# DeltaNet stage of a two-layer decoder step: GpSimd's copies, products and subtractions go to VectorE and ScalarE

## The chip, the cores and the metric

One core of one Trainium2 chip runs the whole step as one program. The metric is device time in microseconds (us) of that program, the median of several runs. Engines are called by the profile's names: PE is TensorE (PEld its weight loads), DVE is VectorE, ACT is ScalarE, POOL is GpSimd, and SP issues all DMAs of this kernel.

## What is computed

A prompt of 256 tokens and 8 sample sequences of 4 tokens go through two decoder layers together (288 columns). Layer 1 mixes its tokens with a gated DeltaNet: 16 heads of 128 x 128, a short convolution on q, k and v, and a chunked form with a triangular inverse. Only this layer is touched. Cut from the reference:

```python
qkv, new_buf = causal_dwconv(qkv, conv_buf, conv_w, None)      # width 4, with the last 3 rows kept
qkv = silu(qkv); q, k, v = split(qkv)                          # 16 heads of 128 each
q = l2norm(q) * DK ** -0.5; k = l2norm(k)
A = where(strict, (k * beta) @ k^T * dec, 0) + I               # per head and chunk
sol = triangular_solve(A, [v * beta, k * beta * exp(gc)])
def step(S, inp):
    v_new = vw_c - kcd_c @ S
    o = qg_c @ S + attn_c @ v_new
    S = S * gl_c[..., None, None] + kg_c^T @ v_new             # the state's update
```

For the samples the state has 8 blocks of 128 x 128 per head (one per sequence), each with its own decay gl.

## The kernel before

**Precision and weights.** Every projection takes operands split into a high and a low part. `wsplit` makes the parts of at most 512 weight columns: ACT copies the high part (`wh`), then the low part `wl = raw - wh` is a subtraction on DVE, or, for every third piece (`pool_share` is 3, counter `wn`), on POOL (L386). PE takes three matmuls of 288 columns per 128 weight columns: `xH,wh`, `xL,wh`, `xH,wl`. The pieces are made a few ahead of their use: five `wh` and five `wl` buffers.

**The DeltaNet stage.** `gdn` runs 16 heads as five streams of jobs: `inputs` (four projections and the convolutions, the filler), `prepare` (transposes, norms, decay products), `invert` (the triangular inverse, `inverse`), `sample` and `sample2` (the 8 sample states), and `chain` (the two prompt chunks). `flow` writes PE's order by hand from a table of latencies, so PE takes its steps in a fixed order and waits in it. The order of DVE, ACT, POOL and SP is set by the framework's scheduler from the program and its own costs. After head 8 the first half of the output projection (`out_half`) joins the filler.

**What POOL does in the stage.** A third of the `wl` pieces; the convolution's small copies in `evac_pad` (history into the padded row `pad`, new history into `osc`, L596 to L600); copies of the sample columns of q and k into `KQx` (L1538, L1539); in `inverse` half of the mask products `at`, the products `a8t`, `sx` and the subtraction `lo`, and the two copies into `X` (L729, L730); the scaling of the sample state `S0` by its decays, one product of 128 x 1024 per head (L1627); the spread of `US` to `UX`, one product of 96 x 1024 per head (L1644); the powers of -0.5 in `rsqrt_small` (L345); zeroing of `pad`; and two of the eight `xL` subtractions in `out_half`.

**The sample state.** `S0` is loaded, read by PE against `KQx`, scaled by POOL, and later gets two PSUM banks of 128 x 512 added (`p_row`, L1653 and L1654) before it is stored. The tag `row` has one PSUM bank.

Of the kernel before, what the change touches and what calls it, by code (L numbers as in the profile page):

```python
# [42 lines left out]
# ---------------------------------------------------------------- host: layout and shape constants  # L43
def _consts():
# [37 lines left out]
    # halved on the chip  # L82
    ("w0", 8), ("a0", 8), ("ka", 8), ("sw", 48), ("sb", 12), ("gw", 192), ("gnorm", 1),
    # as they come
# [24 lines left out]
def _wt(w, pad=None):  # L109
    """(K, C) -> [col tile, 128, ktile*128]"""  # L110
    w = np.asarray(w)
    K, C = w.shape
    return np.ascontiguousarray(w.reshape(K // 128, 128, C // 128, 128).transpose(2, 1, 0, 3)).reshape(
        C // 128, 128, K)
# [8 lines left out]
def _tok(a):  # L123
    """(tokens, features) -> [128, ftile, tokens]"""
    a = np.asarray(a)
    n, f = a.shape
    return np.ascontiguousarray(a.T.reshape(f // 128, 128, n).transpose(1, 0, 2))


def layout(i):  # L130
# [44 lines left out]
    # (b, h, v, k) -> [pair, (half of the sequences, k), (head, sequence of the half), v]  # L175
# [3 lines left out]
    # (b, h, p, n) -> [b, n, h*64+p]  # L179
# [3 lines left out]
    # (b, h, k, v) -> [h, k, b, v]  # L183
# [46 lines left out]
# ---------------------------------------------------------------- the program  # L230
# [19 lines left out]
class K:  # L250
    def __init__(self, tc, ctx, d):
# [10 lines left out]
        self.pe_us, self.step = 0.0, None  # L262
        self.wready = []
        self.wplan()

    # -- small things
    def gt(self, nm="gt"):
        """short-lived [128, N]"""
        return self.mp.tile([128, N], F32, name=nm, tag="gt", bufs=self.ngt)

    def gn(self, nm="gn"):
        """the same, of a later stage"""
        return self.mp.tile([128, N], F32, name=nm, tag="gn", bufs=2)

    def gw(self, nm="gw"):
        """the same for padded rows"""
        return self.mp.tile([128, 320], F32, name=nm, tag="gw", bufs=self.ngw)

    def P(self, tag=None):
        """a PSUM bank; self.pt names the current stage's banks"""  # L280
# [3 lines left out]
    def PA(self):  # L284
        """one of all eight banks"""
# [4 lines left out]
    def reserve(self, pads, dls, gws, gts):  # L290
        """the row buffers come first in a pool: they are free first"""
# [18 lines left out]
    def tr(self, out, a, r=slice(0, 128)):  # L310
        """out = a transposed; a lies on the partitions r"""
# [20 lines left out]

    def rsqrt(self, y, x, t):
        """y = 1/sqrt(x): y, x, t tile views of one shape, on VectorE"""
# [7 lines left out]
    def rsqrt_small(self, y, x):  # L342
        """the same for a few columns, on GpSimd"""
# [3 lines left out]
    def split(self, hi, lo, x, gain=None, eng=None):  # L347
        """hi + lo = x*gain exactly, each in 12 significant bits"""
# [7 lines left out]
    def stack(self, out, x, twin=0, eng=None):  # L356
        """x [32, n] as 96 rows that contract against those of another such x to a product of full
        precision: hi, lo, hi, or for the other one (twin) hi, hi, lo"""
# [13 lines left out]
    # -- weights  # L372
# [7 lines left out]
    def wsplit(self, raw):  # L380
        """at most WC columns of raw as hi, lo"""
# [9 lines left out]
    def wplan(self):  # L391
        """the weights of all projections, in their order: (w, ktiles[, M[, k0]])"""
# [19 lines left out]
    def wcut(self, w, kts, M=128, k0=0):  # L412
        """loads of at most 1024 columns, split in parts of at most WC"""
# [11 lines left out]
    def wnext(self):  # L425
        """the next part of the planned weights as name, hi, lo; the parts after it are on their way"""
# [7 lines left out]
    def proj_g(self, w, hi, lo, kts, M=128, n=N, ps=None, start=True, stop=True):  # L434
        """psum[:M, :n] = sum over ktiles of w[ktile].T @ (hi + lo)[ktile], w: the next of the plan"""
# [24 lines left out]
    # -- several streams of work side by side, in the order in which TensorE shall take them  # L460
    def weave(self, *streams):
        """advance the (name, generator[, most weight]) streams together, each at its own even pace;
        a generator yields the weight of its last step (None: 1)"""
# [13 lines left out]
    def flow(self, *streams):  # L477
        """streams of jobs side by side, in the order in which TensorE shall take their steps. A job is
        (kind, key, generator function, keys of the jobs that come before it); the first stream fills
        the time in which no step of the others has its operands. LAT says when that is: for each kind  # L480
        of job, how long after its start or the step before the operands of a step come, in us"""
# [60 lines left out]
    # -- norms  # L542
# [21 lines left out]
    def last_norm(self, sq):  # L564
        """1/rms by token from sacc and sq, on all partitions of a PSUM bank"""
# [23 lines left out]
    # -- padded projections  # L589
    def evac_pad(self, ps, H, hist, out_state, zero=True):  # L590
        """psum * r into [H zeros | prompt | per sequence: H history, 4 tokens]; state out"""
# [4 lines left out]
        self.g.tensor_copy(smp[:, :, 0:H], hist)  # L596
        self.tt(p[:, H:H + NP], pr(ps), pr(self.rB), MUL)
        self.tt(smp[:, :, H:], sa(ps), sa(self.rB), MUL)
        self.g.tensor_copy(out_state[:, 0:H], p[:, NP:NP + H])
        self.g.tensor_copy(out_state[:, H:].rearrange("p (b t) -> p b t", t=H), smp[:, :, T:])  # L600
        return p, w, smp

    def shift(self, ps, i, out):
        """token shift of projection tile i -> out [128, N]"""
# [9 lines left out]
    def conv_silu(self, ps, hist, out_state, wcols, bias, out, out2=None):  # L614
        """causal conv of width 4 (weights and bias halved) and silu -> out [128, N]"""
# [16 lines left out]
    def softplus(self, x, r, tl):  # L632
        """x[r] <- softplus(x[r]); tl(): temp views of x's shape"""
# [15 lines left out]
    # -- (I - A)^-1, A strictly lower, given A^T; unit matrices side by side in the free dimension  # L649
    def inverse(self, AT, n, top, XT, tag, bank):  # L650
        """AT, XT: [128, n, 128] views; returns the transposed inverse in XT. top: last level.
        The blocks of 32 on the diagonal lie as [128, n, 32], and have a tile of TensorE each"""
# [9 lines left out]
        def times(l, r, w=1):  # L662
            """l^T r, block by block, in a bank"""
# [10 lines left out]

        at, a8t, ac, a8, lo = small("at"), small("a8t"), small("ac"), small("a8"), small("lo")
        sx, mx = small("sx", 2), small("mx", 2)
        m8 = bc(self.c("m8"), sc, 1)
        for i, u in enumerate(q):
            self.tt(at[u], AT[u, :, u], bc(self.c("up")[u], [32, n, 32], 1), MUL, self.g if i % 2 else None)
        self.v.transpose(out=fl(ac), in_=fl(at))  # L680
        self.tt(a8t, at, m8, MUL, self.g)
        self.tt(a8, ac, m8, MUL)
        self.tt(sx[:, :, 32:64], a8, bc(self.c("id32"), sc, 1), ADD, self.g)
        self.tt(lo, ac, a8, SUB, self.g)
        # inside blocks of 8: (1 + A)(1 + A^2)(1 + A^4)
# [14 lines left out]
        # of blocks of 8 in 32: with M = X A', (1 + M)(1 + M^2) X  # L700
# [16 lines left out]
        # blocks of 32 in pairs  # L717
# [9 lines left out]
        if wide:  # L727
            X = self.X64
            self.g.tensor_copy(X[q[0], :, q[0]], xc[q[0]])  # L729
            self.g.tensor_copy(X[q[1], :, q[1]], xc[q[1]])  # L730
# [13 lines left out]
        # the halves  # L744
# [13 lines left out]
    def inverse4(self, AT, n, XT, X, tag, bank):  # L758
        """the same for 4x4 diagonal blocks of n 32x32 matrices on 32 partitions"""
# [24 lines left out]
    # ------------------------------------------------------------ layer 0: RWKV-7  # L784
    def rwkv(self):
# [8 lines left out]
        # the second half of h is not in use yet  # L794
# [21 lines left out]
        def head():  # L816
# [3 lines left out]
            # as 128 rows hi, hi and 64 of lo  # L820
# [9 lines left out]
        def inputs(j, o):  # L830
            """projections of pair j"""
# [5 lines left out]
        def prepare(j, o):  # L837
# [3 lines left out]
            # rows hi, lo of the first map; lo, hi of the second  # L841
# [4 lines left out]
            # kappa = k * k_k stays without its norm; 1/|kappa|^2 scales by token  # L846
# [50 lines left out]
            # rows (half of the sequences, k)  # L897
# [10 lines left out]
            # products inside a chunk: rows (b | k) for the first head, (k | b) for the second  # L908
# [13 lines left out]
            # bonus  # L922
# [10 lines left out]
        def sample(j, o):  # L933
            """token-major copies; one block of 8 sequences of 4"""
# [37 lines left out]
            # rows that meet only their half of the sequences  # L972
# [20 lines left out]
        def sample2(j, o):  # L993
# [21 lines left out]
            # rows hi, lo  # L1015
# [17 lines left out]
        def centre(y, n, rr, va):  # L1033
            """y - its mean over the head, by token; va: variance"""
# [9 lines left out]
        def chain(j, o, prev):  # L1044
            """chunks in order; y token-major, rows (first head | second head)"""
# [67 lines left out]
    # ------------------------------------------------------------ layer 0: SSD  # L1113
    def transpose3(self, p, src):
        """[128, N] -> token-major in p: two prompt tiles and p[:32, 256:384]"""
# [4 lines left out]
    def seq_ends(self, out, x):  # L1120
        """out = (value at the end of its chunk or sequence) - x, on x's partitions"""
# [5 lines left out]
    def end_factors(self, x, tag):  # L1127
        """x [16, N] cumulated logs -> [128, 16, 9]: exp at the ends of prompt chunk 1 and of the sequences"""
# [13 lines left out]
    def row_parts(self, rows, tag="rowp", bufs=1):  # L1142
        """rows 32..48 of the prompt as hi, lo for products that repeat one of them on all partitions,
        and the columns that choose row h"""
# [10 lines left out]
    def sample_decay(self, rows, r0, TOKs):  # L1155
        """[32 s, 16 h, 32 l]: exp(c_l - c_s) inside a sequence for s <= l, else 0; c in rows r0.. of rows"""
# [11 lines left out]
    def ssd(self):  # L1168
# [33 lines left out]
        def first():  # L1202
            """dt and the decay sums; B and C"""
# [5 lines left out]
            # softplus by token, in fewer columns  # L1209
# [26 lines left out]
        def groups():  # L1236
            """B and C"""
# [102 lines left out]
        def group(g, os):  # L1340
# [4 lines left out]
            for b in range(B):  # L1345
                if b % 2 == 0:
                    h2 = al("h0", [128, 2, 512], "Gm")
                    self.load(h2, d["sssd"][b:b + 2, :, gs].rearrange("b p x -> p b x"))
                    # by turns on two blocks of the columns
# [48 lines left out]
    def ssd_gate(self, j):  # L1398
        """silu of z, twice, waits in DRAM"""
# [7 lines left out]
    def layer0(self):  # L1407
        """both groups of heads; the second one's projections fill the end of the first one's chain"""
# [41 lines left out]
    # ------------------------------------------------------------ layer 1: gated DeltaNet  # L1450
    def gdn(self):
# [25 lines left out]
        # beta, decay sums  # L1477
# [37 lines left out]
        def inputs(h, o):  # L1515
            """projections of head h"""
# [18 lines left out]
        def prepare(h, o):  # L1535
            KQ = o.KQ
            kqv = KQx.rearrange("p (b x) -> p b x", x=68)
            self.g.tensor_copy(kqv[:, :, 0:4], sa(KQ[:, 0, :]))  # L1538
            self.g.tensor_copy(kqv[:, :, 32:36], sa(KQ[:, 1, :]))  # L1539
            # k token-major, decays and products inside a chunk  # L1540
# [588 lines left out]
```

## Time and profile before

| | |
|---|---|
| median of 3 runs | 3469.5 us (3468.0 to 3475.63) |
| profiled execution, span | 3472.1 us |
| PE busy in the span | 3343.0 us (96%) |
| DVE, ACT, POOL busy | 2259.5 us (65%), 1653.4 us (48%), 1394.1 us (40%) |
| the DeltaNet stage in the profiled execution | about 1754 to 2466 us |

The profiled execution has no time of its own beside its span of 3472.1 us; it lies 2.6 us above the median. PE's busy time is modelled from pipelined matmuls. A wait names the instruction that ended it. The DeltaNet stage is the 712 us between the first matmuls of its projections and the last head's end.

### The profile page before, as it was taken

Reading aid. Unit: us, or ns where it says so; the run is one execution under the profiler, and the core shown is the slowest. Engines: PE = TensorE matmul, PEld = TensorE weight load, DVE = VectorE, ACT = ScalarE, POOL = GpSimd, SP = SyncE. Lnnn points to the kernel's source line nnn. Section 1 sums busy time; section 2 is a strip of 40 time slices with the busy share of each in tenths; the row PEclk is TensorE's granted clock in tenths of the full one; section 3 lists DMA queues with packets and bytes.
Section 4 is the critical chain, followed back from the end, with each engine's and each line's share of the span. In section 5 each row is a group of like instructions: output and inputs, shape, how many; then the busy total and the mean of one; then the engine's idle time right before and its main releaser. Section 6 shows DMA issues by size and latency. Waiting matters only on the chain. (4 is left out here: it accounts for less than half of the span.)

```text
span 3472.1 us, 73636 instructions
## 1 busy us (share of the span) xinstructions
PE 3343.0 (96%) x27952; PEld 3154.0 (91%) x27952; DVE 2259.5 (65%) x4775; ACT 1653.4 (48%) x3623; POOL 1394.1 (40%) x1899
## 2 busy tenths in 40 slices
PE   8989999899999999999999999999999999999998
PEld 6878788788999999999988888887989999999998
DVE  8666667775765366446577877888667654663563
ACT  6544445544544344444545555555454444443444
POOL 6444443543433233233435444444434332332333
PEclk9999999999999999999999999999999999999999
DMA  7522223566445544554643444444654455455554
GB/s 235 192 89 96 79 92 118 170 211 223 157 166 164 165 164 166 166 166 165 188 140 130 137 137 135 132 135 136 213 205 165 164 166 167 165 165 165 165 167 144
DMA packets 194818, 547.23 MB, mean 158 GB/s; under 512 B 33824, under 2 KB 60064, under 8 KB 194464
## 3 DMA queue, kind: packets, MB, share of 16 engines
q1 hardware_dynamic: 194464, 542.52, 48.0%
q8 instruction: 220, 3.60, 0.4%
q14 instruction: 134, 1.10, 0.1%
HBM read 511.58 MB, written 30.86 MB: 156 GB/s over the span
## 5 line engine op out<-in xcount | busy, mean ns | idle before, releaser
L304 PE MATMUL p_acc<-xH,wh 128*128 128x288 f32 x6464 | 1971.9, 305 | 5.9 <-ACT xH L329 3.8
L304 PE MATMUL p_acc<-xL,wh 128*128 128x288 f32 x6464 | 1919.9, 297 | 3.7 <-DVE xL L316 3.6
L304 PE MATMUL p_acc<-xH,wl 128*128 128x288 f32 x6464 | 1916.4, 296 | 4.1 <-DVE wl L316 4.0
L329 ACT ACTIVATE wh<-raw 128x512 fp32r<-128x512 f32 x1755 | 1094.7, 629 | 1157.7 <-PE p_acc L304 1015.0
L316 POOL TENSOR_TENSOR wl<-raw,wh 128x512 fp32r<-128x512 f32 x585 | 772.6, 1321 | 1334.6 <-ACT wh L329 1289.4
L304 PEld LDWEIGHTS p_acc<-xH,wh 128*128 128x128 f32 x6464 | 1221.1, 189 | 35.4 <-issue 11.6
L304 PEld LDWEIGHTS p_acc<-xH,wl 128*128 128x128 f32 x6464 | 1226.0, 190 | 6.9 <-DVE wl L316 5.2
L304 PEld LDWEIGHTS p_acc<-xL,wh 128*128 128x128 f32 x6464 | 1223.8, 189 | 7.9 <-DVE xL L316 4.9
L316 DVE TENSOR_TENSOR wl<-raw,wh 128x512 fp32r<-128x512 f32 x1170 | 855.4, 736 | 529.9 <-ACT wh L329 503.5
L316 DVE TENSOR_TENSOR pad<-p_acc,rB 128x256 f32<-128x256 f32 x348 | 92.3, 299 | 92.7 <-PE p_acc L304 92.1
L316 POOL TENSOR_TENSOR sacc<-sacc,sq 128x288 f32<-128x288 f32 x104 | 95.0, 914 | 115.8 <-ACT sq L329 84.3
L316 DVE TENSOR_TENSOR h<-p_acc,h 128x288 f32<-128x288 f32 x128 | 57.9, 455 | 127.4 <-PE p_acc L304 127.4
L319 DVE SCALAR_TENSOR_TENSOR fy<-pad,pv,fy 128x304 f32<-128x304 f32 x176 | 128.5, 730 | 5.2
L319 DVE SCALAR_TENSOR_TENSOR cy<-pad,pv,cy 128x312 f32<-128x312 f32 x180 | 117.0, 650 | 6.3 <-ACT cy L329 2.7
L316 DVE TENSOR_TENSOR xL<-fu,xH 128x288 fp32r<-128x288 f32 x88 | 64.3, 730 | 39.2 <-ACT xH L329 39.2
L595 POOL MEMSET pad<- 128x2 f32 (+2 forms) x174 | 17.2, 100 | 179.7 <-DVE fy L319 100.5
L319 DVE SCALAR_TENSOR_TENSOR xL<-h,pv,xH 128x288 fp32r<-128x288 f32 x80 | 66.5, 831 | 24.4 <-ACT xH L329 22.4
L316 DVE TENSOR_TENSOR fu<-fu,fy 128x256 f32<-128x256 f32 (+1 forms) x176 | 81.0, 501 | 1.2
L329 ACT ACTIVATE fy<-fy 128x304 f32<-128x304 f32 x88 | 39.9, 454 | 81.1 <-DVE fy L319 81.1
L316 DVE TENSOR_TENSOR fu<-p_acc,rB 128x288 f32<-128x288 f32 x88 | 40.2, 457 | 55.8 <-PE p_acc L304 55.8
L325 DVE TENSOR_SCALAR fy<-pad,pv 128x304 f32<-128x304 f32 x88 | 65.3, 742 | 1.2
L329 ACT ACTIVATE sq<-h 128x288 f32<-128x288 f32 x90 | 39.8, 442 | 54.3 <-DVE h L316 53.9
(685 smaller groups left out, 3599.6 us busy)
## 6 DMA issues: line engine op xcount, KB each, us to landing
raw<-i_w_fi SPq DMA_DIRECT2D x352, 512.0 KB, 3.6
raw<-i_w_fo SPq DMA_DIRECT2D x160, 512.0 KB, 3.5
raw<-i_w_c SPq DMA_DIRECT2D x128, 512.0 KB, 3.6
raw<-i_w_ab SPq DMA_DIRECT2D x92, 512.0 KB, 3.6
raw<-i_w_oab SPq DMA_DIRECT2D x32, 512.0 KB, 3.9
raw<-i_w_oc SPq DMA_DIRECT2D x32, 512.0 KB, 3.8
raw<-i_w_xkv SPq DMA_DIRECT2D x31, 512.0 KB, 4.3
raw<-i_w_xq SPq DMA_DIRECT2D x16, 512.0 KB, 5.1
```

The costliest lines, as they stand in the source:

```text
L304: i = self.pe.matmul(out, l, r, start=start, stop=stop)
L316: (eng or self.v).tensor_tensor(out=out, in0=a, in1=b, op=op)
L319: self.v.scalar_tensor_tensor(out=out, in0=a, scalar=sc, in1=b, op0=o0, op1=o1)
L325: self.v.tensor_scalar(out=out, in0=a, scalar1=s1, scalar2=s2, op0=o0, op1=o1)
L329: self.s.activation(out=out, in_=a, func=f, scale=scale)
L595: self.g.memset(p[:, 0:H], 0.0)
```

## The change

Inside `gdn` alone (a flag `lone` is set and `pool_share` is 0 while it runs; both are set back after it): all `wl` pieces go to DVE; the small copies of `evac_pad`, `KQx` and `X` go to ACT through `small_copy`; the products and the subtraction of `inverse` go to DVE; `UX` is made by eight ACT instructions of 96 x 128, each with a column of `bsel` as its scale; and the scaling of `S0` is folded into the update, eight DVE instructions of 128 x 128 (`S0 * gl + p`) in place of two additions of 128 x 512. POOL keeps the powers, the zeroing of `pad` and the two `xL` subtractions. `inverse` has the same tag `g` here and another in layer 0, where `lone` is off. The comments are taken out as well, which shifts line numbers by up to 9.

```diff
+    def small_copy(self, out, a):
+        if self.lone:
+            self.act(out, a)
+        else:
+            self.g.tensor_copy(out, a)
@@ evac_pad
-        self.g.tensor_copy(smp[:, :, 0:H], hist)
+        self.small_copy(smp[:, :, 0:H], hist)
...
-        self.g.tensor_copy(out_state[:, 0:H], p[:, NP:NP + H])
+        self.small_copy(out_state[:, 0:H], p[:, NP:NP + H])
...
@@ inverse
+        eng = None if self.lone else self.g
-            self.tt(at[u], AT[u, :, u], bc(self.c("up")[u], [32, n, 32], 1), MUL, self.g if i % 2 else None)
+            self.tt(at[u], AT[u, :, u], bc(self.c("up")[u], [32, n, 32], 1), MUL, eng if i % 2 else None)
-        self.tt(a8t, at, m8, MUL, self.g)
+        self.tt(a8t, at, m8, MUL, eng)
...
@@ sample, sample2
-            self.tt(S0, S0, CD[:, h, 1:9].unsqueeze(2).to_broadcast([128, B, 128]), MUL, self.g)
...
-            self.tt(UX, bc(US.bitcast(F32), [96, B, 128], 1), bc(self.c("bsel", r96), [96, B, 128], 2), MUL, self.g)
+            for b in range(B):
+                self.act(UX[:, b, :], US.bitcast(F32), scale=self.c("bsel", r96)[:, b:b + 1])
...
-                sv = S0[:, 4 * q:4 * q + 4, :].rearrange("p b v -> p (b v)")
-                self.tt(sv, sv, p, ADD)
+                for b in range(4 * q, 4 * q + 4):
+                    self.stt(S0[:, b, :], S0[:, b, :], CD[:, h, 1 + b:2 + b], p[:, b % 4 * 128:b % 4 * 128 + 128], MUL, ADD)
@@ hybrid_step
+            k.pool_share, k.lone = 0, True
             k.gdn()
+            k.pool_share, k.lone = 3, False
```

PE's order is the same row for row in both programs. The orders of DVE, ACT, POOL and SP differ inside the stage alone. On DVE, one head in the middle of the stage, from the product `Aq` of `prepare` into the first steps of `inverse` (`at_g`, `ac_g`, `a8t_g`, `a_g`, `sx_g`, `lo_g`); before:

```order
L316 TENSOR_TENSOR Aq<-p_ma,DEC 128x256
L316 TENSOR_TENSOR at_g<-Atg,cst 32x64 x2
L316 TENSOR_TENSOR wl<-raw,wh 128x512
L319 SCALAR_TENSOR_TENSOR KQ<-ct,cy 128x256
L319 SCALAR_TENSOR_TENSOR KQ<-ct,cy 128x32
L680 STREAM_TRANSPOSE ac_g<-at_g 128x64
L316 TENSOR_TENSOR wl<-raw,wh 128x512
L319 SCALAR_TENSOR_TENSOR Rg<-p_mb,TOKg,X_28451 128x128
L316 TENSOR_TENSOR a_g<-ac_g,cst 128x64
L319 SCALAR_TENSOR_TENSOR Ats<-p_row,nf,Ls 32x32
L316 TENSOR_TENSOR Aqs<-p_row,Ls 32x32
L316 TENSOR_TENSOR c_g<-Ats,cst 32x32 x2
```

and now:

```order
L317 TENSOR_TENSOR Aq<-p_ma,DEC 128x256
L317 TENSOR_TENSOR wl<-raw,wh 128x512
L320 SCALAR_TENSOR_TENSOR KQ<-ct,cy 128x256
L320 SCALAR_TENSOR_TENSOR KQ<-ct,cy 128x32
L317 TENSOR_TENSOR at_g<-Atg,cst 32x64 x4
L320 SCALAR_TENSOR_TENSOR Rg<-p_mb,TOKg,X_28559 128x128
L689 STREAM_TRANSPOSE ac_g<-at_g 128x64
L317 TENSOR_TENSOR a8t_g<-at_g,cst 128x64
L317 TENSOR_TENSOR a_g<-ac_g,cst 128x64
L317 TENSOR_TENSOR wl<-raw,wh 128x512
L317 TENSOR_TENSOR sx_g<-a_g,cst 128x2x32
L317 TENSOR_TENSOR lo_g<-ac_g,a_g 128x64
```

Five small instructions that stood on POOL are now in DVE's row. From `Aq` to the step `xc_g<-sx_g,p_ma` of the inverse, DVE has five `wl` in this head where it had three; in the other heads four or five where it had two or three.

On DVE in the same head, the end of that piece, up to `xc_g`; before:

```order
L319 SCALAR_TENSOR_TENSOR cy<-pad,pv,cy 128x312
L316 TENSOR_TENSOR O<-p_y,qs 128x128
L319 SCALAR_TENSOR_TENSOR S_29246<-S_29095,cd_g,p_mb 128x128
L319 SCALAR_TENSOR_TENSOR KQ<-ct,cy 128x256
L319 SCALAR_TENSOR_TENSOR KQ<-ct,cy 128x32
L672 STREAM_TRANSPOSE xt_g<-p_ma 128x64
L316 TENSOR_TENSOR xc_g<-sx_g,p_ma 128x64
```

and now:

```order
L320 SCALAR_TENSOR_TENSOR cy<-pad,pv,cy 128x312
L317 TENSOR_TENSOR O<-p_y,qs 128x128
L320 SCALAR_TENSOR_TENSOR S_29365<-S_29215,cd_g,p_mb 128x128
L680 STREAM_TRANSPOSE xt_g<-p_ma 128x64
L317 TENSOR_TENSOR xc_g<-sx_g,p_ma 128x64
L320 SCALAR_TENSOR_TENSOR KQ<-ct,cy 128x256
L320 SCALAR_TENSOR_TENSOR KQ<-ct,cy 128x32
```

Here, and in 7 of the 16 heads, `xt_g` and `xc_g` have moved ahead of the two `KQ`.

On ACT, the same head, around the spread of the sample update (`US` to `UX`) and the copies `yc_g` and `X` of the inverse; before:

```order
L329 ACTIVATE wh<-raw 128x512
L329 ACTIVATE US<-uds 32x128 x2
L329 ACTIVATE ct<-cy 128x312
L329 ACTIVATE wh<-raw 128x512
L329 ACTIVATE yc_g<-p_ma 32x64
L329 ACTIVATE wh<-raw 128x512
L329 ACTIVATE X_22181<-p_ma 32x2x32
```

and now:

```order
L330 ACTIVATE wh<-raw 128x512
L330 ACTIVATE US<-uds 32x128 x2
L330 ACTIVATE ct<-cy 128x312
L330 ACTIVATE UX<-US,cst 96x128 x8
L330 ACTIVATE yc_g<-p_ma 32x64
L330 ACTIVATE X_22181<-ac_g 32x2x32 x2
L330 ACTIVATE wh<-raw 128x512 x2
```

Eight instructions for `UX` and the two copies into `X` now stand in front of `yc_g` and of the next pieces of `wh`.

## Rows read from the trace of the kernel before

**Rows 1.** The stage's stretch: length, busy us (count) by engine, clock, DMA share, GB/s.

```profile
1754.00:2466.00 712.00, 663.85 (x6385) 597.66 (x6384) 567.99 (x1540) 373.48 (x1079) 328.00 (x501) 0.98 0.42 137
```

**Rows 2.** What PE waited for in that stretch: total us, times, longest.

```profile
PE p_ma L304 <- DVE xc_g L316: 12.2, 7, 2.1
PE p_mb L304 <- DVE ud L323: 10.9, 11, 1.7
PE p_ma L304 <- DVE ac_g L316: 4.6, 6, 0.9
PE p_ma L304 <- DVE yc_g L725: 4.2, 5, 1.3
PE p_acc L304 <- DVE wl L316: 4.0, 2, 2.0
```

**Rows 3.** Groups on POOL there: count, busy us, mean ns, idle before.

```profile
L316 POOL TENSOR_TENSOR wl<-raw,wh 128x512 fp32r<-128x512 f32 x94 | 123.3, 1312 | 149.1 <-ACT wh L329 145.0 <-PE p_row L304 2.3 <-issue 1.1
L316 POOL TENSOR_TENSOR UX<-US,cst 96x1024 fp32r<-96x1024 f32 x16 | 33.2, 2074 | 10.3 <-DVE US L316 7.5 <-ACT US L329 2.1 <-DVE O L316 0.4
L316 POOL TENSOR_TENSOR S<-S,cd_g 128x1024 f32<-128x1024 f32 x16 | 32.5, 2034 | 0.7 <-PE p_row L304 0.7
L345 POOL TENSOR_TENSOR r<-x,mhalf 128x6 f32<-128x6 f32 x16 | 21.3, 1329 | 52.5 <-DVE x L323 37.7 <-PE p_acc L304 14.5
```

**Rows 4.** One POOL instruction in time: start, length.

```profile
2218.80 2.19 POOL L316 TENSOR_TENSOR S<-S,cd_g 128x1024 f32<-128x1024 f32 x1
```

**Rows 5.** DVE in the same five microseconds: start, length.

```profile
2218.70 0.53 DVE L319 SCALAR_TENSOR_TENSOR cy<-pad,pv,cy 128x312 f32<-128x312 f32 x1
2219.35 1.98 DVE L319 SCALAR_TENSOR_TENSOR cy<-pad,pv,cy 128x312 f32<-128x312 f32 x1
2223.18 0.18 DVE L316 TENSOR_TENSOR xc_g<-sx_g,p_ma 128x64 f32<-128x64 f32 x1
```

**Rows 6.** PE's next matmul after that, with the idle time before it in us.

```profile
2223.50 0.30 PE L304 MATMUL p_ma<-xc_g,xt_g 32*32 32x32 f32 x13 [1.65 <-DVE xc_g L316]
```

**Rows 7.** Groups on DVE in the stage, as rows 3.

```profile
L316 DVE TENSOR_TENSOR wl<-raw,wh 128x512 fp32r<-128x512 f32 x188 | 154.3, 821 | 39.8 <-ACT wh L329 38.0 <-PE p_y L304 0.2
L319 DVE SCALAR_TENSOR_TENSOR cy<-pad,pv,cy 128x312 f32<-128x312 f32 x144 | 95.4, 663 | 3.8 <-ACT cy L329 2.7
L316 DVE TENSOR_TENSOR S<-S,p_row 128x512 f32<-128x512 f32 x32 | 21.9, 684 | 3.3 <-PE p_row L304 2.9
L323 DVE TENSOR_SCALAR ud<-u,TOKg 128x128 f32<-128x128 f32 x32 | 17.3, 540 | 9.1 <-ACT u L329 9.0
L323 DVE TENSOR_SCALAR uds<-us,TOKg 32x128 f32<-32x128 f32 x16 | 5.6, 349 | 0.1
L319 DVE SCALAR_TENSOR_TENSOR S<-S,cd_g,p_mb 128x128 f32<-128x128 f32 x16 | 5.2, 327 | 0.4 <-PE p_mb L304 0.4
```

**Rows 8.** Single instructions of DVE there: ns shortest/median/longest.

```profile
L316 DVE TENSOR_TENSOR wl<-raw,wh x188: 637/691/2402, 1755.1 to 2464.3; 128x512 fp32r<-128x512 f32 x188
L319 DVE SCALAR_TENSOR_TENSOR cy<-pad,pv,cy x144: 489/532/2202, 1769.0 to 2399.2; 128x312 f32<-128x312 f32 x144
L323 DVE TENSOR_SCALAR ud<-u,TOKg x32: 232/286/1692, 1844.3 to 2465.0; 128x128 f32<-128x128 f32 x32
L323 DVE TENSOR_SCALAR uds<-us,TOKg x16: 258/268/997, 1825.8 to 2440.3; 32x128 f32<-32x128 f32 x16
L316 DVE TENSOR_TENSOR a_g<-ac_g,cst x16: 206/213/977, 1810.9 to 2425.1; 128x64 f32<-128x64 f32 x16
```

**Rows 9.** Four us after a wait of PE; columns as rows 1.

```profile
1898.00:1902.00 4.00, 4.00 (x35) 3.68 (x35) 2.64 (x12) 1.47 (x3) 1.21 (x2) 0.59 0.42 135
```

**Rows 10.** Groups on ACT in the stage, as rows 3.

```profile
L329 ACT ACTIVATE wh<-raw 128x512 fp32r<-128x512 f32 x282 | 175.4, 627 | 132.3 <-PE p_acc L304 123.2 <-ACT ct L329 2.4 <-issue 1.5
L329 ACT ACTIVATE X<-p_row,inv 128x128 f32<-128x128 f32 x32 | 9.7, 353 | 0.0
L329 ACT ACTIVATE mx_g<-p_ma 128x64 f32<-128x64 f32 x16 | 3.6, 223 | 14.1 <-DVE xt_g L672 14.1
```

More of the change, by code (lines that the diff above doesn't have):

```diff
@@ L262, in __init__ @@
         self.pe_us, self.step = 0.0, None
+        self.lone = False
         self.wready = []
@@ L595, in evac_pad @@
         self.g.memset(p[:, 0:H], 0.0)
-        self.g.tensor_copy(smp[:, :, 0:H], hist)
+        self.small_copy(smp[:, :, 0:H], hist)
         self.tt(p[:, H:H + NP], pr(ps), pr(self.rB), MUL)
         self.tt(smp[:, :, H:], sa(ps), sa(self.rB), MUL)
-        self.g.tensor_copy(out_state[:, 0:H], p[:, NP:NP + H])
-        self.g.tensor_copy(out_state[:, H:].rearrange("p (b t) -> p b t", t=H), smp[:, :, T:])
+        self.small_copy(out_state[:, 0:H], p[:, NP:NP + H])
+        self.small_copy(out_state[:, H:].rearrange("p (b t) -> p b t", t=H), smp[:, :, T:])
         return p, w, smp
@@ L678, in inverse @@
         for i, u in enumerate(q):
-            self.tt(at[u], AT[u, :, u], bc(self.c("up")[u], [32, n, 32], 1), MUL, self.g if i % 2 else None)
+            self.tt(at[u], AT[u, :, u], bc(self.c("up")[u], [32, n, 32], 1), MUL, eng if i % 2 else None)
         self.v.transpose(out=fl(ac), in_=fl(at))
-        self.tt(a8t, at, m8, MUL, self.g)
+        self.tt(a8t, at, m8, MUL, eng)
         self.tt(a8, ac, m8, MUL)
-        self.tt(sx[:, :, 32:64], a8, bc(self.c("id32"), sc, 1), ADD, self.g)
-        self.tt(lo, ac, a8, SUB, self.g)
+        self.tt(sx[:, :, 32:64], a8, bc(self.c("id32"), sc, 1), ADD, eng)
+        self.tt(lo, ac, a8, SUB, eng)
         yield
@@ L728, in inverse @@
             X = self.X64
-            self.g.tensor_copy(X[q[0], :, q[0]], xc[q[0]])
-            self.g.tensor_copy(X[q[1], :, q[1]], xc[q[1]])
+            self.small_copy(X[q[0], :, q[0]], xc[q[0]])
+            self.small_copy(X[q[1], :, q[1]], xc[q[1]])
         p = self.P(bank)
@@ L1537, in prepare @@
             kqv = KQx.rearrange("p (b x) -> p b x", x=68)
-            self.g.tensor_copy(kqv[:, :, 0:4], sa(KQ[:, 0, :]))
-            self.g.tensor_copy(kqv[:, :, 32:36], sa(KQ[:, 1, :]))
+            self.small_copy(kqv[:, :, 0:4], sa(KQ[:, 0, :]))
+            self.small_copy(kqv[:, :, 32:36], sa(KQ[:, 1, :]))
             KT_ = o.KT = mp.tile([128, 2, 128], F32, name="KTt", tag="KTt", bufs=2)
```

## The prediction

> **What bounds the kernel now.** I first read the busy times by stretch, because the change acts in one stretch only. In the DeltaNet stage, 712 us, PE is busy 663.85 us, DVE 567.99, ACT 373.48 and POOL 328.00 [rows 1]. PE sets the pace and is idle 712 - 663.85 = 48 us. What the stage can give back is those 48 us, and what the clock loses: the granted clock is 0.98, so about 0.02 x 712 = 14 us of full-speed time are missing. [...]
>
> Next, what PE waits for: nearly always a DVE instruction, `xc_g` 12.2 us, `ud` 10.9, `ac_g` 4.6, `yc_g` 4.2, `wl` 4.0 [rows 2], which is 36 of the 48 us. So the question is why DVE is late while it is idle a fifth of the stage. The order in time shows it. POOL starts scaling `S` at 2218.80 and takes 2.19 us [rows 4]; DVE's `cy`, started at 2219.35, takes 1.98 us where its twin just before took 0.53, and ends when POOL ends (2221.0 against 2221.3) [rows 4, 5]. The inverse's `xc_g` stands behind it in DVE's row, and PE then waits 1.65 us for it [rows 6]. The same instruction has a median of 532 ns and a longest of 2202 [rows 8].
>
> How much of this there is: count times (mean - median). `wl`: 188 x (821 - 691) = 24 us; `cy`: 144 x (663 - 532) = 19; `ud`: 32 x (540 - 286) = 8 [rows 7, 8]. I count twenty DVE groups with more than 1 us of it, from `wl` down to `uds`, 16 x (349 - 268) = 1.3 [rows 7, 8]; together they make about 100 us, of DVE's 568 busy us.
>
> **The change part by part.**
>
> *The stretching goes.* POOL's subtractions (123.3 us), `UX` (33.2) and the scaling of `S` (32.5) [rows 3] and all its copies leave. The powers stay, 16 of 1329 ns for `r` [rows 3] and as many shorter ones, mostly at moments when DVE itself waits for them. I leave 5 us for them: DVE gets back 95 us of its 100. Bounds: 100, and none if DVE's long times had another reason, which the match of ends in rows 4 and 5 speaks against.
>
> *What DVE takes over.* 94 pieces of `wl` at 691 ns [rows 3, 8]: 65 us. The state's update: eight instructions of 128 x 128 from PSUM with a scalar column, of which DVE has the same form at 327 ns, for two at 684 [rows 7]: 16 x (8 x 0.327 - 2 x 0.684) = 20 us. Five small ones per head in the inverse, at the 213 ns of `a_g`, which has the shape of most of them [rows 8]: 17 us. Sum 102 us. So **DVE's load in the stage stays as it is**, 568 - 95 + 102 = 575 us, with bounds of 555 (all 100 back, and a seventh of the added time lost in overlap of neighbours) and 670 (nothing back). What changes is where it lies: 1 to 2 us blocks that fall on any instruction are replaced by pieces under 0.7 us whose place the order sets.
>
> [...]
>
> *What that is worth to PE, wait by wait.* `xc_g` and `ud`, 23 us together [rows 2]: both stand behind the scaling of `S`. In that piece of a head DVE gets back about 1.45 us at `cy` [rows 5] and about 0.6 at the instructions that meet a POOL `wl` (half of its 1312 ns, [rows 3]), but has two more `wl` and the five small ones in front of `xc_g`: 2 x 0.69 + 5 x 0.21 = 2.4 us of durations, some 2.0 when neighbours overlap. This is nearly even. But in 7 heads `xc_g` has moved ahead of the two `KQ`, which is worth some 0.6 us, and a `wl` ahead of `Aq` is no longer stretched. I take 23 down to 9, since both together are over 1 us of the 1.3 that a wait has on average (23 us, 18 times). `ac_g` and `yc_g`, 8.8 us: behind `UX` (2074 ns [rows 3]) and a stretched `wl`; 2 to 2.5 us come back, one `wl` of 0.69 is added. I take 9 down to 2. `wl` at the stage's start, 4.0 us: two blocks of some 1.1 us go, about three more `wl` come; 4 down to 3. The other 12 us of small waits I leave. Sum: 14 + 7 + 1 = 22 us. Bounds: 0 if the added work fills every gap that opens, 36 if all five waits go.
>
> *The clock.* The 14 us missing are as much as nine dips like that of rows 9, at 1.6 us each. A dip follows a long wait of PE, and rows 2 have longest waits of 1.3 to 2.1 us; fewer of those, fewer dips. I take four of nine: 6 us back, bounds 0 and 14.
>
> *ACT takes over* eight `UX` instructions per head, 144 small copies of the convolution, and four copies per head into `KQx` and `X`. `UX` at the 353 ns of `X<-p_row,inv` (128 x 128 with a scale column), copies at the 223 ns of `mx_g` [rows 10]: 16 x 8 x 0.353 = 45, plus (144 + 64) x 0.223 = 46; 91 us. ACT goes from 373 to about 465 of 690 us. The cover: ACT waits 123.2 us of the stage for PE to free a `wh` buffer [rows 10], so it is ahead, by up to five pieces of 12 matmuls. A matmul of the stage takes 0.10 us on average (664 us over 6385, [rows 1]), so five pieces are 6 us. A row of eight `UX`, 2.8 us, in front of `yc_g` and two pieces of `wh` is within that. `yc_g` waits in ACT's row for `UX` and so for `US`, but `US` itself comes about 1 us earlier when no `wl` of POOL blocks it. I charge 1 us in all, with bounds 0 and 16 x 1 (a whole us late at each head). If that cover were gone, each `UX` row would cost PE its 2.8 us, 45 us in all.
>
> [...]
>
> *SP.* The store of `S` comes one weight load earlier in its row. The update ends some 0.5 us later (8 x 0.327 against 2 x 0.684, minus overlap), so SP may wait there with one load behind it; three `raw` buffers hide it. Nothing charged; a whole us at each head would be 16 us, but only if the buffers had run dry, and PE's largest waits name no `raw` load [rows 2].
>
> Sum: 22 + 6 - 1 = 27 us. The profiled execution's span of 3472.1 us becomes 3445; it lies 2.6 us above the median of the runs, so I expect a median of 3469.5 - 27 = 3442.5, **3443 us**.
>
> **The rivals.**
>
> *All five waits go.* If the order places the moved work where DVE is idle (712 - 568 = 144 us of the stage), PE gets 36 us and the dips with them, 14: 3469.5 - 50 = 3419. For it: blocks of 1.5 to 2 us like that of rows 5 are as long as the longest waits [rows 2]. Against: between `Aq` and `xc_g` DVE is given about as much as it gets back.
>
> *It evens out.* DVE's load does not fall, POOL's help of 94 pieces beside it is lost, and PE waits as long for the same instructions, now behind `wl`. Gains and losses within 7 us: 3463 to 3476. For it: 95 against 102 us. Against: a block hits the critical instruction with its full length, a piece of `wl` is there only if the order puts it.
>
> *Slower: DVE held at the head of its row.* DVE takes its instructions in order, and a `wl` whose `wh` is not yet there holds all behind it: now 38.0 us over 188 pieces [rows 7], 0.2 us each. With 94 pieces more, and several in a row after the state's update, each head would get 5.9 x 0.2 = 1.2 us of holding plus the added work in front of the inverse (2.4 us), against 2 us back: 1.6 us per head, 25 us with a few more dips: 3495. It decides once three or more added `wl` stand in front of `xc_g` or `ud` without their `wh`. Against: `wh` is made ahead, as PE's freeing of buffers shows.
>
> *The change doesn't reach its end.* GpSimd still reads SBUF for its powers. If each of the 31 blocked an instruction on PE's path for its whole length, 1.3 us for `r`, the 36 us of waits would stay, and the time would be that of the second rival. Against: DVE mostly waits for these powers and has nothing to block.
>
> **How the numbers follow.** A measurement of this kernel can tell about 0.2%, 7 us, from no change. The forecast, a gain of 10 to 38 us, has 0.56; everything goes 0.18; evens out 0.14 (part of it just beyond 7 us on either side); slower 0.12. Faster by over 0.2%: 0.76; within: 0.12; slower: 0.12. The range reaches from the full gain, 3418, to just past even, 3474; it leaves out the slower case and the edges.
>
> **What would show it.** Right: no DVE `cy`, `ud`, `wl` far over its median; DVE's busy time in the stage near 575 less the shorter stage's share, POOL under 60; PE's waits for `xc_g`, `ud`, `ac_g`, `yc_g` about a third of 32 us; fewer stretches with a clock under 1. Wrong: the same total of waits with DVE's durations at their medians (then the order, not the blocking, was the cost); or new waits of PE for `wl`, `XTg` or ACT's `yc_g`.

## The result, and the profile after

The changed kernel takes 3416.03 us (median of 4 runs, 3415.37 to 3424.91) beside 3468.75 for the kernel before: a ratio of 0.9854 over all runs (0.9848 by the medians), interval 0.984 to 0.9867. It is faster by 53 us, twice the 27 that were forecast, and almost exactly the first rival, 3419.

The trace of the changed kernel is of the slowest of its four runs, 3424.91 us, span 3423.1; the other three lie within 1 us of 3416. Set against the traced 3472.1 us before, it accounts for 49 of the 53 us. Nearly all of them are in the DeltaNet stage, whose last store begins at 2418.4 us and not at 2466.2. The stage's stretch, columns as in [rows 1]:

```profile
1754.00:2418.00 664.00, 652.93 (x6405) 590.40 (x6406) 543.75 (x1814) 438.58 (x1414) 44.08 (x89) 0.99 0.47 147
```

PE's idle time was 712 - 663.85 = 48 us and is 664 - 652.93 = 11: 37 us are waits that are gone. PE's busy time for the same matmuls fell from 663.85 to 652.93: the other 11 us are the clock. Added up over four-us slices of the stage, the granted clock lost 13.8 us of full-speed time before and loses 3.4 now; of slices under 0.95 there were 12 and are 3. What PE still waits for in the stage, as [rows 2]:

```profile
PE p_acc L305 <- DVE wl L317: 3.3, 3, 2.4
PE p_row L305 <- PE p_ma L305: 2.1, 7, 0.3
PE p_row L313 <- DVE S L320: 1.0, 1, 1.0
PE p_acc L305 <- ACT xH L330: 0.9, 1, 0.9
...
PE p_mb L305 <- DVE ud L324: 0.3, 1, 0.3
```

`xc_g`, `ac_g` and `yc_g` are gone from the list, and `ud` has 0.3 us of its 10.9. Single instructions of DVE in the stage, ns shortest/median/longest, as [rows 8] (the last count of a line is of every second instruction where there are more than 200):

```profile
L317 DVE TENSOR_TENSOR wl<-raw,wh x281: 635/682/694, 1758.4 to 2416.6; 128x512 fp32r<-128x512 f32 x141
L320 DVE SCALAR_TENSOR_TENSOR cy<-pad,pv,cy x144: 489/532/546, 1769.9 to 2350.6; 128x312 f32<-128x312 f32 x144
L324 DVE TENSOR_SCALAR ud<-u,TOKg x32: 232/280/290, 1840.4 to 2417.2; 128x128 f32<-128x128 f32 x32
```

The medians stand where they stood (532 ns for `cy`), and the long ones are gone: `cy`'s longest was 2202 ns and is 546. The costs of the moved work, groups on DVE, then ACT, then POOL, as [rows 3], [rows 7] and [rows 10]:

```profile
L317 DVE TENSOR_TENSOR wl<-raw,wh 128x512 fp32r<-128x512 f32 x281 | 188.7, 680 | 28.3 <-ACT wh L330 26.4
L320 DVE SCALAR_TENSOR_TENSOR S<-S,cd_g,p_row 128x128 f32<-128x128 f32 x128 | 36.9, 342 | 1.0 <-PE p_row L305 0.6
...
L330 ACT ACTIVATE wh<-raw 128x512 fp32r<-128x512 f32 x282 | 174.3, 627 | 114.4 <-PE p_acc L305 107.9 <-DMA raw<-i_w_c 1.5 <-issue 1.2
L330 ACT ACTIVATE UX<-US,cst 96x128 fp32r<-96x128 f32 x128 | 39.0, 387 | 0.0
L330 ACT ACTIVATE osc<-pad 128x24 f32<-128x24 f32 x48 | 10.6, 221 | 4.5 <-DVE pad L317 4.1
...
L353 POOL TENSOR_TENSOR r<-x,mhalf 128x6 f32<-128x6 f32 x16 | 21.3, 1333 | 213.3 <-DVE x L324 213.3
```

One head on DVE, from `Aq` to the inverse's `xc_g`, in order of time (start, length, both us):

```profile
2182.33 0.42 DVE L317 TENSOR_TENSOR Aq<-p_ma,DEC 128x256 f32<-128x256 f32 x1
...
2185.06 0.18 DVE L317 TENSOR_TENSOR a8t_g<-at_g,cst 128x64 f32<-128x64 f32 x1
2185.17 0.22 DVE L317 TENSOR_TENSOR a_g<-ac_g,cst 128x64 f32<-128x64 f32 x1
2185.32 0.68 DVE L317 TENSOR_TENSOR wl<-raw,wh 128x512 fp32r<-128x512 f32 x1
2185.92 0.22 DVE L317 TENSOR_TENSOR sx_g<-a_g,cst 128x64 f32<-128x64 f32 x1
2186.05 0.22 DVE L317 TENSOR_TENSOR lo_g<-ac_g,a_g 128x64 f32<-128x64 f32 x1
...
2191.88 0.17 DVE L317 TENSOR_TENSOR xc_g<-sx_g,p_ma 128x64 f32<-128x64 f32 x1
```

Neighbours overlap: a `wl` of 0.68 us holds its successor back by 0.60, a small product of 0.18 or 0.22 by 0.11 to 0.15. And the piece is even from head to head. From `Aq`'s start to `xc_g`'s start it was 8.99 to 13.05 us before, 10.41 in the mean of 16 heads; now it is 8.44 to 9.55, mean 9.03.

### The profile page after: what moved, and what is told of

Same layout as the page of the kernel before. It is cut to its first block, busy times and chain, and to the rows that moved or that the text cites. A ratio compares the mean times of both kernels' runs of the same rounds, so it can differ in the third digit from the quotient of the medians.

```text
span 3423.1 us, 73588 instructions
## 1 busy us (share of the span) xinstructions
PE 3330.2 (97%) x27952; PEld 3144.8 (92%) x27952; DVE 2236.6 (65%) x5045; ACT 1718.5 (50%) x3959; POOL 1108.8 (32%) x1485
## 4 chain that ended last, share of the span: by engine, by line
PE 73%; DVE 2%; ACT 1%; issue 1%; DMA 1%; POOL 0%; SPq 0%; DVEq 0%; ACTq 0%; POOLq 0%
PE p_acc L305 66%; PE p_ma L305 3%; PE p_mb L305 2%; PE p_row L305 1%; PE p_y L305 1%; DVE wl L317 0%; PE p_row L313 0%; ACT wh L330 0%; DVE h L317 0%; PE p_mb L313 0%; DMA cache<-i_cv 0%; DMA xres<-i_xT 0%; PE p_ma L313 0%; DVE xL L320 0%; ACT xH L330 0%
## 5 line engine op out<-in xcount | busy, mean ns | idle before, releaser
L317 DVE TENSOR_TENSOR wl<-raw,wh 128x512 fp32r<-128x512 f32 x1264 | 891.5, 712 | 517.6 <-ACT wh L330 492.7
L317 POOL TENSOR_TENSOR wl<-raw,wh 128x512 fp32r<-128x512 f32 (+1 forms) x491 | 649.8, 1323 | 1210.5 <-ACT wh L330 1168.8
L320 DVE SCALAR_TENSOR_TENSOR cy<-pad,pv,cy 128x312 f32<-128x312 f32 x180 | 97.9, 544 | 4.6 <-ACT cy L332 2.0
L353 POOL TENSOR_TENSOR r<-x,mhalf 128x6 f32<-128x6 f32 x16 | 21.3, 1333 | 213.3 <-DVE x L324 213.3
L339 POOL COPY ost<-pad 128x2 f32<-128x2 f32 (+1 forms) x176 | 60.6, 375 | 59.7 <-DVE pad L317 59.7
```

Source lines behind the costliest of these rows:

```text
L317: (eng or self.v).tensor_tensor(out=out, in0=a, in1=b, op=op)
L320: self.v.scalar_tensor_tensor(out=out, in0=a, scalar=sc, in1=b, op0=o0, op1=o1)
L339: self.g.tensor_copy(out, a)
L353: self.g.tensor_tensor(out=y, in0=x, in1=self.mhalf[0:x.shape[0], 0:n], op=ALU.pow)
```

## The experiments

Three theories. **A**: a GpSimd instruction that reads SBUF stretches VectorE's instructions with two SBUF inputs, and these blocks made PE wait; the gain is their going. (In e5's expectation it is called A1.) Rival **A2**: it is GpSimd being busy at all, or its writes. Rival **B**: the gain comes from order and balance, that is, fewer steps that hop between engines and better places for the work. Times are differences to the kernel before in the same series (medians 3465.15 for e1 to e4, 3466.75 for e5 to e8, 3464.51 for e9 to e12, 3468.75 for the changed kernel); between series the kernel before differs by up to 4 us, and what follows across series is good to no more than that.

| run | what it is | us | difference | ratio, interval |
|---|---|---|---|---|
| changed kernel | | 3416.0 | -53 | 0.984 to 0.9867 |
| e1 | a third of `wl` back on GpSimd | 3449.1 | -16 | 0.9929 to 0.9967 |
| e2 | scaling of `S0` back on GpSimd | 3424.7 | -40 | 0.986 to 0.9898 |
| e3 | added: 94 idle reads by GpSimd | 3471.1 | +6 | 1.0003 to 1.0026 |
| e4 | before, with `wl` moved alone | 3441.4 | -24 | 0.9908 to 0.995 |
| e5 | added: idle writes by GpSimd | 3421.7 | -45 | 0.9853 to 0.9884 |
| e6 | `UX` back on GpSimd | 3415.8 | -51 | 0.9828 to 0.9879 |
| e7 | small copies and inverse's products back | 3411.5 | -55 | 0.9824 to 0.9864 |
| e9 | `wl` and state alone | 3421.6 | -43 | 0.9852 to 0.9893 |
| e8 | changed kernel, and layer 0 likewise | 3394.7 | -72 | 0.9775 to 0.9806 |
| e10 | e9, and `wl` in layer 0 | 3401.9 | -63 | 0.9796 to 0.9849 |
| e11 | e7, and layer 0 likewise | 3393.2 | -71 | 0.9772 to 0.9813 |
| e12 | e11, and no `wl` on GpSimd anywhere | 3384.0 | -81 | 0.9745 to 0.9795 |

### What blocks: GpSimd's reads, its writes, or its being busy (e3, e5)

Both are the changed kernel with idle work added on GpSimd beside every third `wl`, into a tile that nobody reads. e3 repeats the subtraction (two SBUF inputs, 1.3 us). e5 reads a single column and then writes 128 x 1280, 1.17 us.

```diff
+        if self.lone and self.wn % 3 == 1 and n == WC:
+            self.tt(self.spare, raw, wh.bitcast(F32), SUB, self.g)                  # e3
+            self.g.tensor_copy(self.spare[:, 0:1], wh[:, 0:1].bitcast(F32))         # e5
+            self.g.memset(self.spare, 0.0)                                          # e5
```

> The changed kernel with all its work where it is, and in addition GpSimd makes every third wl piece a second time into a tile that nobody reads: the same instruction as before on GpSimd, for nothing. Theory A: DVE's wl, cy, ud are stretched to 1.2 us and more where they meet it; 3428 to 3450 us. Rival B (moved work, shorter hand-overs and the new order brought the gain): 3414 to 3420.

> As the run in which GpSimd makes every third wl again for nothing, but it reads only one column of wh (to wait for the same moment) and then fills a tile of 128x1280 with zeros, about as long and without reading SBUF. Theory A1 (reading SBUF blocks DVE): DVE's wl and cy stay at their medians, 3416 to 3426 us, a few us of it from powers that queue behind. Theory A2 (a busy GpSimd, whatever it does, is enough: its queue delays the powers that DVE waits for): near the reading run, 3450 to 3471.

e3 measured 3471: it gives back the whole gain, more than either theory had asked. e5 measured 3422 with GpSimd as long at work (178.94 us of 712 in e3, 188.56 of 664 in e5). Two places in e3, POOL first, then DVE (start, length):

```profile
2174.84 1.26 POOL L317 TENSOR_TENSOR spare<-raw,wh 128x512 f32<-128x512 f32 x1 [3.38 <-issue]
...
2187.10 1.72 POOL L317 TENSOR_TENSOR spare<-raw,wh 128x512 f32<-128x512 f32 x1 [1.89 <-issue]
```

```profile
2174.89 1.28 DVE L317 TENSOR_TENSOR sx_g<-a_g,cst 128x64 f32<-128x64 f32 x1
...
2187.00 0.69 DVE L317 TENSOR_TENSOR wl<-raw,wh 128x512 fp32r<-128x512 f32 x1
```

At 2174.84 POOL is first, and DVE's 0.22 us product lasts 1.28 us, until POOL ends (2176.17 against 2176.10). At 2187.00 DVE is first; its `wl` keeps its 0.69, and POOL takes 1.72 where its median is 1.30. In both places the instruction that started second is the one that takes longer. In e5, the same two views:

```profile
2177.98 1.17 POOL L399 MEMSET spare<- 128x1280 f32 x1
...
2187.13 1.17 POOL L399 MEMSET spare<- 128x1280 f32 x1
```

```profile
2177.95 0.68 DVE L317 TENSOR_TENSOR wl<-raw,wh 128x512 fp32r<-128x512 f32 x1
2178.55 0.22 DVE L317 TENSOR_TENSOR sx_g<-a_g,cst 128x64 f32<-128x64 f32 x1
...
2187.16 1.46 DVE L324 TENSOR_SCALAR O<-O,fac 128x128 f32<-128x128 f32 x3
```

Under the first write `sx_g` takes its 0.22 us. Under the second, three `O<-O,fac` take 1.46 us; in e3, clear of GpSimd, they took 0.66. Single instructions of DVE, e3 and then e5, show the same for the whole stage:

```profile
L317 DVE TENSOR_TENSOR wl<-raw,wh x279: 635/683/1790, 1756.4 to 2462.3; 128x512 fp32r<-128x512 f32 x140
L320 DVE SCALAR_TENSOR_TENSOR cy<-pad,pv,cy x144: 490/534/1665, 1762.1 to 2394.8; 128x312 f32<-128x312 f32 x144
```

```profile
L317 DVE TENSOR_TENSOR wl<-raw,wh x279: 637/683/695, 1757.5 to 2414.8; 128x512 fp32r<-128x512 f32 x140
L320 DVE SCALAR_TENSOR_TENSOR cy<-pad,pv,cy x144: 489/533/545, 1758.6 to 2345.6; 128x312 f32<-128x312 f32 x144
L324 DVE TENSOR_SCALAR ud<-u,TOKg x32: 231/285/1000, 1829.2 to 2411.9; 128x128 f32<-128x128 f32 x32
```

So the two runs show two kinds of blocking. e3's subtractions, which read SBUF, stretch instructions with two SBUF inputs (`wl` to 1790 ns, `cy` to 1665), and e5's writes do not: `wl` and `cy` keep their times (longest 695 and 545). Writes still stretch the products with a scalar column from SBUF to SBUF: in e5's stage `ud` to 1000 ns, where the changed kernel's longest is 290, and the three `O<-O,fac` above from 0.66 to 1.46 us.

e5 is 6 us slower than the changed kernel, 8 by the differences, and that is all that is left for A2. What these few us are stays open: PE waits 0.3 us for `ud` in both, and DVE waits no longer for GpSimd's powers (22.4 us for `r` against 22.0).

Can e3's 55 us come from anything but the blocks? Not from the order: read in order of time, DVE's 1799 instructions of the stage stand in the same order as in the changed kernel. The extra read keeps the `raw` and `wh` buffers longer, but none of PE's waits names a DMA or POOL, and DVE waits no longer for `wh` than in the changed kernel (22.7 us against 26.4). What rises is DVE's durations in the stage, count by mean added over all groups, from 647 to 704 us, and PE's idle time, from 11 to 712 - 661.88 = 50. The first of the two places shows how one becomes the other. The next instruction of DVE that PE needs there is `Aqs`, the last to read the one PSUM bank of `row`; the stretched `sx_g` stands in front of it (DVE, then PE with its idle time):

```profile
2176.40 0.17 DVE L317 TENSOR_TENSOR Aqs<-p_row,Ls 32x32 f32<-32x32 f32 x1
```

```profile
2176.67 1.09 PE L305 MATMUL p_row<-S,KQx 128*64 128x128 f32 x16 [1.91 <-issue]
```

The profile names no releaser ("issue"), but PE starts 0.10 us after the end of `Aqs`. At this step PE waits 16.3 us in e3's stage, where it was 2.1 in the changed kernel ("PE p_ma" is PE's own step before; the end of `Aqs` fits for these too):

```profile
PE p_row L305 <- PE p_ma L305: 7.7, 10, 0.8
PE p_row L305 <- issue: 7.6, 4, 1.9
PE p_row L305 <- DVE Aqs L317: 1.0, 1, 1.0
```

For `xc_g` PE does not wait at all in e3, and for `ud` 0.7 us. So e3 shows what blocks cost, but not at the places where they cost most in the kernel before: which instruction a block hits depends on where GpSimd's work lies.

### Which part of the change counts (e1, e4, e2, e9, e6, e7)

```diff
-            k.pool_share, k.lone = 0, True
+            k.pool_share, k.lone = 3, True        # e1; in the kernel before, pool_share = 0 alone is e4
+            k.pool_share, k.lone = 0, False       # e7
```

> The changed kernel, but every third wl piece is again subtracted on GpSimd. Theory A (GpSimd instructions that read SBUF lengthen DVE instructions, and that is what PE waited for): DVE has 65 us less work in the stage, but wl and cy are stretched again; 3430 to 3450 us. Rival B (DVE's load and order set the time, the stretching is harmless): DVE is relieved, 3400 to 3416.

> The kernel before with one part of the change: all wl pieces of the stage on VectorE, the rest of GpSimd's work stays. Theory A: less than half of the blocking goes (123 of 328 us of GpSimd) and DVE gets 65 us of work: 3440 to 3460 us. Rival B: only DVE's added load counts, 3470 to 3500.

`wl` alone is worth 24 us, and 33 when it is undone: theory A's numbers both times. e1 is also the case against a balance of loads. Its DVE has less to do than the changed kernel's (durations of 629 us against 647, as the 94 `wl` are elsewhere), and it is 33 us slower. By rival B's balance it had to gain. The slower pieces of GpSimd (a `wl` takes 1.29 us there in the median, 0.69 on DVE) are not what holds it up: no wait of PE names POOL. DVE's order differs too in e1, so e3 is the cleaner case.

```diff
+            self.tt(S0, S0, CD[:, h, 1:9].unsqueeze(2).to_broadcast([128, B, 128]), MUL, self.g)   # e2
...
+            self.tt(UX, bc(US.bitcast(F32), [96, B, 128], 1), bc(self.c("bsel", r96), [96, B, 128], 2), MUL, self.g)   # e6
```

> The changed kernel, but the sample state is again scaled by GpSimd in one product of 128x1024 and updated by two additions of 128x512. Theory A: one block of 2 us per head on cy or what stands there, waits of PE for xc_g and ud come back; 3424 to 3440 us. Rival B: DVE has 20 us less work; 3410 to 3417.

e2 also has the two additions of 128 x 512 back. It loses 9 us (12 by the differences), and what PE waits for tells where (total, times, longest; single instruction of DVE below it):

```profile
PE p_mb L305 <- DVE ud L324: 14.9, 12, 1.3
```

```profile
L324 DVE TENSOR_SCALAR ud<-u,TOKg x32: 255/282/1536, 1829.0 to 2414.2; 128x128 f32<-128x128 f32 x32
```

The scaling of `S0` is the block that stands behind `ud`: seven of the 32 last 1.38 to 1.54 us, each while the scaling runs. e9 takes the change's two large parts alone, `wl` and the state:

> Two parts of the change alone: all wl pieces of the stage on DVE, and the state's scaling folded into the update. UX, the small copies and the inverse's small steps stay on GpSimd. If these two are the whole gain, 3408 to 3420 us; if all parts are needed together, 3422 to 3435.

3421.6 lies between the two expectations: 43 of the 53 us. On top of e4 the state is worth some 19 us, against 9 to 12 when it alone is undone. PE's waits for `xc_g` are 12.9 us in e4 and 2.5 in e9, those for `ud` 5.0 and none. The parts do not add.

> The changed kernel, but the spread of US to UX is again one product of 96x1024 on GpSimd. Theory A: one block of 2 us per head falls on Vf, wl or US, in front of ac_g and yc_g; 3420 to 3432 us. Rival C (eight UX in ACT's row hold up wh and yc_g): 3408 to 3415, faster without them.

> The changed kernel, but the small copies of the convolution, of KQx and X and the five small steps of the inverse are again on GpSimd; wl, UX and the state stay where the change put them. Theory A: their blocks are 0.2 to 0.5 us, so the stretching is small; what comes back is mostly the slower hand-over of the inverse: 3418 to 3430 us. Rival: ACT without 208 small copies is faster, 3408 to 3415.

Theory A's range was missed both times: neither undoing costs anything that can be measured. e6 lies between its two ranges. e7's 3411.5 is in the range of its rival (ACT faster without the copies), but by the differences it is 2 us from the changed kernel, less than the series can tell. In e6 the blocks are back, as the longest of `cy` and of `wl` show, and PE's waits do not care (single instructions of DVE, then one of PE's waits):

```profile
L320 DVE SCALAR_TENSOR_TENSOR cy<-pad,pv,cy x144: 489/532/1950, 1754.7 to 2337.0; 128x312 f32<-128x312 f32 x144
L317 DVE TENSOR_TENSOR wl<-raw,wh x283: 636/683/2255, 1753.7 to 2418.0; 128x512 fp32r<-128x512 f32 x142
```

```profile
PE p_ma L305 <- DVE yc_g L734: 0.8, 1, 0.8
```

With the rest of the blocks gone, the slack in front of `yc_g` covers one of 2 us per head. Where the small copies are on GpSimd too, `UX` on ACT seems worth something: e7 against e9 is 3411.5 against 3421.6, with intervals that just overlap. How much of that is `UX` stays open. The moves of the small copies and of the inverse's products brought nothing: e7, without them, is not slower than the changed kernel.

### The same cure elsewhere (e8, e10, e11, e12)

Layer 0 has the same third of `wl` on GpSimd. e8 sets both flags there too, e10 and e11 apply parts, and e12 takes every remaining `wl` from GpSimd.

```diff
+        k.pool_share, k.lone = 0, True            # e8 and e11; lone stays False in e10
         k.layer0()
+        k.pool_share, k.lone = 3, False           # e12: 0, False, and 0 from the start
```

> The changed kernel, and in layer 0 too all wl pieces go to DVE, the small copies to ACT and the inverse's small steps to DVE, while the other GpSimd work of layer 0 stays. Theory A: waits of PE in layer 0 shrink, 3395 to 3412 us. Rival B: DVE's added load counts, 3418 to 3435.

> The same two parts in the DeltaNet stage, and in layer 0 the wl pieces alone go to DVE. If layer 0's 21 us come from wl too, 3386 to 3400 us; if they come from its small copies and the inverse's steps, 3408 to 3418.

> In the DeltaNet stage wl, UX and the state as in the changed kernel, small copies and the inverse's steps on GpSimd (3411.5 us so far); layer 0 with wl on DVE and its small copies and the inverse's steps off GpSimd. If the parts add up, 3386 to 3394 us.

> The run before, and no wl piece on GpSimd anywhere in the program, so in the memory stage, the output projections, the cross-attention and the ConvFFN too. In the long stretches where PE has no idle time it should change nothing; a few us in the memory stage and at the borders: 3378 to 3394 us. If DVE's added load counts where it is 55% busy, 3395 or more.

Layer 0 gives another 18 to 21 us (e8 against the changed kernel, e10 against e9, e11 against e7), and e10 has them with `wl` alone, so it is `wl` there as well. Two ranges were missed narrowly: e8 is 0.3 us below theory A's, and e10 lies 2 us above the range for `wl` alone. The rest of the program gives another 9 (e12 against e11, with intervals that overlap). e12 ran in 3384.0 us, a ratio of 0.977: it beats the changed kernel by 32 us.

## Why the prediction was right or wrong

**The mechanism was right.** Stretched instructions of DVE are the cause: e3 brings them back with DVE's order kept and loses the whole gain, e5 keeps GpSimd as busy almost without reads and loses 6 to 8 us. Most signs that were named for "right" are there: `cy`, `ud` and `wl` within 4% of their medians, POOL at 44 us (under 60 was said), fewer stretches with a low clock, no new wait of PE for `wl`, `XTg` or `yc_g`. Two went further than was said: PE's waits for the four DVE steps are 0.3 us and not a third of 32, and DVE's busy time is under its bound. "Faster" had been given 0.76. The size was missed: 3416 is 27 us under the forecast and 2 us under the low end of the range, 3418, which had been set where all five waits and all dips are gone and left nothing for the small waits.

**The term that was mis-sized is PE's waits:** 22 us forecast, 37 measured, past the bound of 36 that was given for all five going. `xc_g` and `ud` gave 23 where 14 had been taken, `ac_g` and `yc_g` 9 where 7, `wl` 0.7 where 1, and the small waits, which had been left as they were, nearly 5. The step that failed is "between `Aq` and `xc_g` DVE is given about as much as it gets back", which left 9 of the 23 us of `xc_g` and `ud`. The piece became 1.38 us shorter per head, 22 us in 16 heads, and nearly all 23 us went. Both sides of the step were off.

- What was added was charged at 2.0 us. In the mean a head has 4.3 `wl` there where it had 2.75: 1.56 by 0.60 is 0.9, and five small products by 0.11 to 0.15 are 0.65. Together 1.6, minus 0.2 for the two `KQ` (0.43 us) that went behind in 7 of 16 heads: 1.4. Durations had been priced, and the order counts by the distance from one start to the next.
- So what came back was 1.38 + 1.4 = 2.8 us and not 2.05. In the mean the excess over the median was 0.6 at `cy`, 0.5 at `ud`, 0.4 at `wl` and 0.8 at smaller instructions, and DVE's own idle time fell by 0.3. `ud` and most of the small ones had been left out of the sum for this piece.

**What the piece tells of PE's waits.** In the kernel before PE waited for `ud` or `xc_g` in each of the 16 pieces: 0.2 to 1.0 us in the four under 9.2 us, 1.7 to 2.5 in the five over 11. Summed rightly, the mean was a fair guide: 22 us shorter in all, nearly 23 us of waits gone. But the length alone does not set the wait. Pieces of 9.1 us still cost up to 1.0 before, while those of 9.5 cost at most 0.3 now.

**The clock:** 6 us forecast, 11 measured, within 0 and 14. The 1.6 us of a dip are 0.41 x 4, from [rows 9]; there the clock is 0.50 for the three us from 1898, behind PE's wait of 1.85 us for `xc_g`. The loss went with the waits, as the prediction had it (12 slices under 0.95 became 3), and so was too small with them.

**DVE's load** was to be 575 us and is 543.75, under the lower bound of 555. The durations hardly changed (651 to 647, forecast +7, so 11 us off), but 274 more instructions overlap 20 us more with their neighbours (83 us before, 103 now: durations less busy time). e1 shows that this load was not what the time hung on.

**ACT** was charged 1 us and cost nothing that shows: it still waits 107.9 us for PE, and PE waits for it 0.9 us. `UX` costs 39.0 / 128 = 0.305 us apiece in a row, 2.4 for eight, where 0.353 and 2.8 were priced; a single one lasts 387 ns. The copies, at 221 ns, cost what `mx_g` had told. For the state's update the 327 ns of the row became 342, and in busy time it is 36.9 / 128 = 0.288 us apiece.

**The rivals.** "All five waits go" is nearly what happened: four went, the wait for `wl` is still 3.3 of 4.0 us, and the small waits made up for it. Its price, 3419, was within 3 us. It was given 0.18 because of the step above. "Evens out" had rested on 95 against 102 us of DVE, a balance that does not decide. "Held at the head of its row" fell: DVE's waits of `wl` for `wh` went from 38.0 us over 188 pieces to 26.4 over 281, so there is no more holding although there are more pieces. "GpSimd still reads for its powers" fell too: no `wl`, `cy`, `ud` or `O<-O,fac` is over 694, 546, 290 or 288 ns in the changed kernel's stage. DVE waits for those powers (22.0 us for `r`) and has nothing to block.

## What to carry to other kernels

Here work on GpSimd that reads SBUF was not free help beside a loaded VectorE (in e3 it cost 55 us, with results that nobody reads): compare the longest with the median of one form of VectorE instruction, look whether the long ones end when a GpSimd instruction ends, and move the reading work even if VectorE's own list gets longer by it. Move the large pieces first and measure: here two parts had 43 of 53 us, and small copies nothing. Price moved instructions by the distance from start to start (0.60 us for a `wl` that lasts 0.68), and in a piece between two steps of the critical engine count the excess of every form, not of the largest alone.

## What the runs showed of the hardware

- A memset on GpSimd, which reads nothing, leaves VectorE's `wl` and `cy`, with two SBUF inputs, at their times (longest 695 and 545 ns in e5) and yet stretches its products with a scalar column from SBUF to SBUF (`ud` from a median of 285 to 1000 ns in e5's stage). I had expected writes to be harmless.
- The changed kernel has one such place of its own, just behind the stage: under a fill of 128 x 2304 on GpSimd, three `O<-O,fac` take 1.97 us instead of 0.66.
- The blocking goes both ways: with VectorE first, a GpSimd subtraction took 1.72 us where the median is 1.30.
- 94 idle subtractions of 1.3 us, whose results nobody reads, cost 55 us of 3416 (59 by the differences), with VectorE's order unchanged.
